# Step-size projection of the Mamba-2 layer: fp32 on four 32-column groups of TensorE and a stacked identity, in place of a slab whose columns are repeated four times

## Chip, cores and metric

The kernel runs on one core of one Trainium2 chip. The metric is the device time of one execution in microseconds (us), as the median of several runs. Lower is better.

## What is computed

The reference is one inference step of a two-layer streaming encoder: layer 0 mixes tokens by chunked band attention, layer 1 by a Mamba-2 scan, and a dense MLP follows each. There are 512 prompt tokens and 64 sample tokens, so 576 columns in all, in two halves of 288. The change concerns one product in layer 1, the 32 columns of the input projection that give each head its step size.

```python
proj = x @ w_in                                  # 1024 -> z, x/B/C, dt
z = proj[..., :D_INNER]
xbc = proj[..., D_INNER:D_INNER + CONV_CH]
dt_raw = proj[..., D_INNER + CONV_CH:]           # 32 columns, one per head
...
dt = jax.nn.softplus((dt_raw + dt_bias).astype(jnp.float32)).reshape(bsz, t, g, r)
a = -jnp.exp(a_log.astype(jnp.float32)).reshape(g, r)
y, h = _ssd_scan(xs, dt, a, bm, cm, h0)
```

## The kernel before

**Weights.** `Weights` walks through 223 slabs of 128x1024 in the order of `weight_plan`. SyncE's queue (SP) loads each into one of four raw buffers `wr`. `split` makes two fp32r halves of it, `wh` by a ScalarE cast (L182) and `wl` by a VectorE subtraction (L183), in one of five pairs of buffers. Every large product is then three fp32r matmuls for each of eight slices of the inner dimension: `wh` by `xh`, `wh` by `xl`, `wl` by `xh`. `dense` (L308) does both halves of the tokens for each weight, `dense_half` (L338) one half only.

**The order of the work.** The program is written in one sequence, and the scheduler of the language places the instructions of each engine in an order of its own, by readiness and priority; an engine then works through its list in order. Two helpers interleave: `side.start` takes a generator, and `side.tick` runs a piece of it every so many matmuls. So a layer norm runs in pieces between matmuls. A step whose result is used late can still be queued early.

**The place of the change.** `in_proj(0)` (from L917) begins the Mamba layer. For half 0 and then half 1 it computes dt (32 columns, `dense_half([dtw], h)`), c and b, then x0 and x1 of the first group. The slab `dt` holds the 32 columns four times side by side, so that it has 128 like all others; only the first 32 rows of its product are used. Half 0 begins while the layer norm of half 1 still runs as side work:

- `layer_norm` (L396) takes sums that GpSimd has made (L393), forms the mean by an fp32 matmul with a constant matrix (L401), squares on ScalarE (L408), adds the squares on VectorE (L412, L413), and gets the scale through `split_stats` (L362) and `bcast` (six matmuls, L372). VectorE multiplies it in (L423), ScalarE adds gain and bias tile by tile (L429, which gives `x32`), ScalarE or VectorE casts to `xh` (L434, L436), and VectorE forms `xl` (L437).
- `dt_in` (L985, VectorE) adds the bias, once for each half. `dt_chain` (L990 to L1004) is the softplus on 32 partitions by 576 columns, one exponential on ScalarE (L991) and some 16 VectorE instructions. The scheduler interleaves them with the convolution steps on VectorE (`conv`, L913).
- The gate slabs z0 and z1 follow (`gate_in`, `dense`), and with z1 as side work `dt_rest`: ten transposes of dt and dt times a on TensorE (L1010, L1011), cumulative sums (L1017, L1018), and the exponentials. The scan of the groups follows (L1071, L1087, L1102), with the projections of the next groups between.

```python
dt_in(dense_half([dtw], h)[0], h)
if h == 1:
    W.drop()
    dt_chain()
```

Of the kernel before, what the change touches and what calls it, by code (L numbers as in the profile page):

```python
# [5 lines left out]
F32 = mybir.dt.float32  # L6
# [7 lines left out]
P = 128  # L14
# [3 lines left out]
HALF = 288  # L18
# [16 lines left out]
PM_ID = PM_D + 16  # L35
# [75 lines left out]
def build(nc, io):  # L111
    from contextlib import ExitStack
    plan = weight_plan()
    with tile.TileContext(nc) as tc, ExitStack() as es:
        V, S, PE, GP, SY = nc.vector, nc.scalar, nc.tensor, nc.gpsimd, nc.sync
# [9 lines left out]
        def tmp(w=NT):  # L125
            return tp.tile([P, w], F32, name="tmp", tag="tmp")
# [4 lines left out]
        def mmt():  # L131
            return pmm.tile([P, 1024], F32, name="mm", tag="mm")
# [11 lines left out]
        x32 = xp.tile([P, 8, NT], F32, name="x32")  # L144
# [3 lines left out]
        class Weights:  # L148
# [37 lines left out]
            def produce(self, i):  # L186
                p = plan[i]
                r = self.raw_free
                if p[0] != "ups":
                    self.split(i, self.raw.pop(r))  # L190
                    self.raw_free += 1
                    return
                r1, r2 = self.raw[r], self.raw[r + 1]
                lo, hi = slice(0, HALFK), slice(HALFK, 1024)
                eng = V if p[2:4] == (0, PLAIN // 2) else GP
                if p[4] == 2:
                    eng.tensor_tensor(out=r2[:, lo], in0=r1[:, lo], in1=r2[:, lo], op=ALU.subtract)  # L197
                    self.split(i, r2)
                    eng.tensor_tensor(out=r2[:, hi], in0=r2[:, hi], in1=r2[:, lo], op=ALU.subtract)  # L199
                    eng.tensor_tensor(out=r2[:, lo], in0=r1[:, lo], in1=r2[:, hi], op=ALU.add)  # L200
                elif p[4] == 4:
                    self.split(i, r2[:, lo])
                elif p[4] == 1:
                    self.split(i, r1)
                    eng.tensor_tensor(out=r1[:, hi], in0=r1[:, hi], in1=r2[:, hi], op=ALU.subtract)
                else:
                    self.split(i, r2[:, hi], r1[:, hi])
                    del self.raw[r], self.raw[r + 1]
                    self.raw_free += 2
                    self.prefetch()  # L210
# [78 lines left out]
        pm = cst.tile([P, PM_N], F32, name="pm")  # L289
# [41 lines left out]
        def dense_half(ws, h):  # L331
            ps = mmt()
            outs = [ps[:, 512 * j:512 * j + HALF] for j in range(len(ws))]
            for k in range(8):
                for w, o in zip(ws, outs):
                    wh, wl = wk(w)(k)
                    for i, (a, b) in enumerate(((wh, xh), (wh, xl), (wl, xh))):
                        PE.matmul(o, a, b[:, k, h * HALF:(h + 1) * HALF],  # L338
                                  start=k == 0 and i == 0, stop=k == 7 and i == 2)
                    side.tick(3)  # L340
            return outs

        def wk(w, n=128, off=0):
            return lambda k: (w[0][:, k * n + off:k * n + off + 128], w[1][:, k * n + off:k * n + off + 128])
# [537 lines left out]
        def ssm():  # L882
            cumd = dr.tile([32, NT], F32, name="cumd")
            expd = dr.tile([32, NT], F32, name="expd")
            with tc.tile_pool(name="ssm", bufs=2) as ap:
                tok = ap.tile([P, 5, 64], F32, name="tok", bufs=1)
                win = ap.tile([P, 5, 32], F32, name="win", bufs=1)
                cumt = ap.tile([P, 5, 32], F32, name="cumt", bufs=1)
# [31 lines left out]
                def in_proj(g):  # L920
                    items = [("c", g, 24 + g, "c"), ("b", g, 16 + g, "b"), ("x", 2 * g, 2 * g, "x0"),
                             ("x", 2 * g + 1, 2 * g + 1, "x1")]
                    out = []
                    if g == 0:
                        ws, xr = [], []
                        dtw = W.get("dt")
                        for h in range(2):
                            if h == 0:
                                side.start(layer_norm(1, 1, False), LN_EVERY)
                            else:  # L930
                                side.drain()
                            dt_in(dense_half([dtw], h)[0], h)
                            if h == 1:
                                W.drop()
                                dt_chain()
                            for i0 in range(0, 4, PAIR_IN):
                                if h == 0:
                                    for i in range(i0, i0 + PAIR_IN):
                                        ws.append(W.get(*items[i][:2]))
                                        xr.append(xpad4(i))  # L940
                                        conv_pre(xr[i], items[i][2])
                                for i, src in zip(range(i0, i0 + PAIR_IN), dense_half(ws[i0:i0 + PAIR_IN], h)):
                                    conv_in(xr[i], src, h * HALF, (h + 1) * HALF)
                                    if h == 1:
                                        W.drop()
                                        out.append(conv(xr[i], items[i][2], items[i][3]))
                        out.append(gate_in(0, 0))
                        side.start(dt_rest(), DE)
                        out.append(gate_in(0, 1))
                        side.drain()  # L950
                        return out
                    res = {}
                    for (kind, j) in GORD:
                        if kind == "z":
                            res["z", j] = gate_in(g, j)
                            continue
                        _, idx, ct, tag = items[{"c": 0, "b": 1, "x": 2 + j}[kind]]
                        w = W.get(kind, idx)
                        xr = xpad()
                        conv_pre(xr, ct)  # L960
                        ps = mmt()
                        dense(ps, wk(w), ax_h, ax_l, 8, (0, 1))
                        conv_in(xr, ps[:, PS0:PS0 + NT], 0, NT)
                        W.drop()
                        res[kind, j] = conv(xr, ct, tag)
                    return [res[k] for k in (("c", 0), ("b", 0), ("x", 0), ("x", 1), ("z", 0), ("z", 1))]
# [10 lines left out]
                def xpad4(i):  # L977
                    if i < 2:
                        return xpad()
                    return ap.tile([P, 2, NT], F32, name="yy", tag="yy", bufs=2).rearrange("p a b -> p (a b)")[:, 0:582]  # L980

                dtt = [ap.tile([P, NT], F32, name=f"dt{i}", tag=("yh", "yl")[i % 2], bufs=4)[0:32] for i in range(4)]

                def dt_in(src, h):
                    V.tensor_scalar(out=dtt[0][:, h * HALF:(h + 1) * HALF], in0=src[0:32], scalar1=hpm[:, 0:1],  # L985
                                    scalar2=None, op0=ALU.add)

                def dt_chain():
                    xr, e, q, p = dtt
                    V.scalar_tensor_tensor(out=e, in0=xr, scalar=-1.0, in1=xr, op0=ALU.mult, op1=ALU.max)  # L990
                    S.activation(e, e, AF.Exp, scale=-1.0)  # L991
                    V.tensor_scalar(out=xr, in0=xr, scalar1=0.0, scalar2=None, op0=ALU.max)
                    V.tensor_scalar(out=q, in0=e, scalar1=2.0, scalar2=None, op0=ALU.add)
                    V.reciprocal(q, q)
                    V.tensor_tensor(out=e, in0=e, in1=q, op=ALU.mult)
                    V.tensor_tensor(out=q, in0=e, in1=e, op=ALU.mult)
                    V.tensor_scalar(out=p, in0=q, scalar1=1.0 / 15.0, scalar2=None, op0=ALU.mult)
                    for c in (13, 11, 9, 7, 5, 3):
                        V.scalar_tensor_tensor(out=p, in0=p, scalar=1.0 / c, in1=q, op0=ALU.add, op1=ALU.mult)
                    V.scalar_tensor_tensor(out=p, in0=p, scalar=1.0, in1=e, op0=ALU.add, op1=ALU.mult)  # L1000
                    V.scalar_tensor_tensor(out=p, in0=p, scalar=2.0, in1=xr, op0=ALU.mult, op1=ALU.add)
                    na = sp.tile([32, 1], F32, name="na", tag="na", bufs=1)
                    S.activation(na, hpm[:, 1:2], AF.Exp)
                    V.tensor_scalar(out=q, in0=p, scalar1=na, scalar2=-1.0, op0=ALU.mult, op1=ALU.mult)  # L1004
# [293 lines left out]
```

## Time and profile before

| | |
|---|---|
| median of 3 runs | 1705.39 us (1703.11 to 1706.24) |
| the profiled execution, its own time | 1701.69 us |
| its span in the trace | 1699.9 us |
| mean granted TensorE clock | 0.991 |
| TensorE matmul (PE) busy | 97% |
| TensorE weight load (PEld) busy | 93% |
| VectorE (DVE) busy | 63% |
| ScalarE (ACT) busy | 46% |
| GpSimd (POOL) busy | 22% |

The profile is taken from one execution, whose own time lies a little below the runs'. The span goes from the first to the last recorded instruction. A share of busy time is an average over the whole span; a stage of 25 us can look quite different. A granted clock of 1.00 is 2.4 GHz, 0.50 is 1.2 GHz.

### The profile page before, as it was taken

How to read it: one execution, taken by the hardware profiler on the slowest of the kernel's cores; microseconds unless marked ns; L12 is line 12 of the kernel's file. 1: busy time of each engine (PE TensorE's matmuls, PEld its weight loads, DVE VectorE, ACT ScalarE, POOL GpSimd, SP SyncE). 2: the span in 40 equal slices, each digit the busy share in tenths (PEclk: the TensorE clock that was granted, in tenths of full speed). 3: DMA queues.
4: the chain of work that ended last, by engine and by line, in shares of the span. 5: the costliest groups of instructions: out<-in, count | busy, mean ns of one | idle time of the engine just before them, and what ended most of it. 6: DMA issues, size and time to landing. Idle time of an engine off the chain costs nothing. (4 is left out here: it accounts for less than half of the span.)

```text
span 1699.9 us, 30804 instructions
## 1 busy us (share of the span) xinstructions
PE 1652.7 (97%) x12545; PEld 1576.5 (93%) x12545; DVE 1064.4 (63%) x1879; ACT 774.8 (46%) x1278; POOL 378.1 (22%) x412
## 2 busy tenths in 40 slices
PE   9999999899999999989999999999998999999995
PEld 8888887899999999989899999999988999999995
DVE  6555556784362736477875775777778637364446
ACT  5433443374261716246663563565326616254332
POOL 0000000211312212206541340344220212131211
PEclk9999999999999999999999999999999999999998
DMA  8333332114131313113332332333211313223121
GB/s 272 106 119 113 111 105 72 62 30 133 51 125 51 123 52 127 61 66 119 117 104 87 103 99 89 99 103 110 68 57 36 125 50 111 64 75 124 52 73 56
DMA packets 76925, 157.22 MB, mean 92 GB/s; under 512 B 11440, under 2 KB 40240, under 8 KB 76784
## 3 DMA queue, kind: packets, MB, share of 16 engines
q1 hardware_dynamic: 76784, 155.25, 28.2%
q8 instruction: 99, 1.62, 0.4%
q14 instruction: 42, 0.34, 0.1%
HBM read 145.80 MB, written 9.42 MB: 91 GB/s over the span
## 5 line engine op out<-in xcount | busy, mean ns | idle before, releaser
L182 ACT CAST wh<-wr 128x1024 fp32r<-128x1024 f32 (+1 forms) x301 | 280.7, 938 | 472.3 <-PE mm L308 362.0
L183 DVE TENSOR_TENSOR wl<-wr,wh 128x1024 fp32r<-128x1024 f32 (+1 forms) x301 | 359.9, 1200 | 106.1 <-ACT wh L182 100.9
L308 PE MATMUL mm<-xh,wl 128*128 128x288 f32 x1088 | 237.8, 299 | 0.0
L308 PE MATMUL mm<-xh,wh 128*128 128x288 f32 x1088 | 237.5, 300 | 0.1
L308 PE MATMUL mm<-xl,wh 128*128 128x288 f32 x1088 | 237.4, 299 | 0.0
L308 PE MATMUL mm<-hh,wl 128*128 128x288 f32 x960 | 222.0, 297 | 0.0
L308 PE MATMUL mm<-hl,wh 128*128 128x288 f32 x960 | 221.7, 296 | 0.0
L308 PE MATMUL mm<-hh,wh 128*128 128x288 f32 x960 | 221.7, 296 | 0.0
L384 DVE TENSOR_TENSOR x<-x,mm 128x288 f32<-128x288 f32 (+1 forms) x112 | 64.5, 580 | 196.2 <-PE mm L308 185.1
L308 PEld LDWEIGHTS mm<-xl,wh 128*128 128x128 f32 x1088 | 174.3, 189 | 4.1 <-issue 3.8
L308 PEld LDWEIGHTS mm<-xh,wh 128*128 128x128 f32 x1088 | 174.5, 188 | 2.6 <-issue 1.4
L308 PEld LDWEIGHTS mm<-xh,wl 128*128 128x128 f32 x1088 | 174.3, 189 | 1.5
L308 PEld LDWEIGHTS mm<-hh,wl 128*128 128x128 f32 x960 | 160.1, 188 | 0.1
L308 PEld LDWEIGHTS mm<-hh,wh 128*128 128x128 f32 x960 | 160.1, 188 | 0.1
L308 PEld LDWEIGHTS mm<-hl,wh 128*128 128x128 f32 x960 | 160.1, 188 | 0.0
L541 PE MATMUL ax<-xh,wh 128*128 128x288 f32 x416 | 123.1, 296 | 0.5 <-ACT ut L559 0.4
L541 PE MATMUL ax<-xl,wh 128*128 128x288 f32 x416 | 122.6, 295 | 0.0
L541 PE MATMUL ax<-xh,wl 128*128 128x288 f32 x416 | 122.5, 294 | 0.0
L197 POOL TENSOR_TENSOR wr<-wr 128x512 f32<-128x512 f32 x24 | 40.7, 1695 | 337.9 <-DMA wr<-in_wts 297.8
L913 DVE SCALAR_TENSOR_TENSOR tmp<-xpad,pm,tmp 128x579 f32<-128x579 f32 x90 | 88.9, 988 | 1.5 <-ACT tmp L911 0.8
L338 PE MATMUL mm<-xh,wh 128*128 128x288 f32 x240 | 72.8, 307 | 8.3 <-DVE xh L434 5.1
L541 PEld LDWEIGHTS ax<-xh,wh 128*128 128x128 f32 x416 | 78.1, 188 | 1.6 <-ACT ut L559 1.3
(267 smaller groups left out, 3503.2 us busy)
## 6 DMA issues: line engine op xcount, KB each, us to landing
wr<-in_wts SPq DMA_DIRECT2D x223, 512.0 KB, 3.4
cumb<-cumd SPq DMA_DIRECT2D x32, 256.0 KB, 3.8
e<-expd SPq DMA_DIRECT2D x48, 64.0 KB, 3.5
tb<-in_rel SPq DMA_DIRECT2D x16, 160.0 KB, 3.0
out_k<-tmp SPq DMA_DIRECT2D x8, 288.0 KB, 2.5
out_v<-tmp SPq DMA_DIRECT2D x8, 288.0 KB, 2.1
tb<-in_rel SPq DMA_DIRECT2D x16, 144.0 KB, 2.9
ts<-in_rel SPq DMA_DIRECT2D x16, 144.0 KB, 3.0
```

What stands on the lines that cost most here:

```text
L182: S.copy(hi[:, sl], raw)
L183: V.tensor_tensor(out=lo[:, sl], in0=raw, in1=hi[:, sl].bitcast(F32), op=ALU.subtract)
L197: eng.tensor_tensor(out=r2[:, lo], in0=r1[:, lo], in1=r2[:, lo], op=ALU.subtract)
L308: PE.matmul(ps[:, o:o + HALF], w, a(k)[:, t0:t0 + HALF], start=first and i == 0, stop=last and i == 2)
L338: PE.matmul(o, a, b[:, k, h * HALF:(h + 1) * HALF], start=k == 0 and i == 0, stop=k == 7 and i == 2)
L384: V.tensor_tensor(out=dst, in0=dst, in1=src, op=ALU.add)
L541: chain(PE.matmul(out, a, b, start=not more and k == 0 and i == 0, stop=k == 3 and i == 2, skip_group_check=True), k or i or name != "t3")
L913: V.scalar_tensor_tensor(out=acc, in0=xr[:, k:k + 579], scalar=col(k), in1=acc, op0=ALU.mult, op1=ALU.add)
```

## The change

The `dt` slab is no longer split. Its raw fp32 buffer is multiplied as it stands, with the fp32 `x32` instead of `xh` and `xl` (`dt_proj`, new). Each of the eight slices of the inner dimension uses 32 columns of the slab as weights and writes to one of four groups of 32 partitions of a PSUM tile, slice k to group k modulo 4, so that each group sums two slices. ScalarE then copies the four partial sums to SBUF, and a matmul with `stack`, four 32x32 identities one under the other, adds them. `stack` is loaded by four small DMAs on SP's queue ahead of the layer. The bias add takes its input from this last product.

```diff
--- before.py
+++ after.py
@@ -186,6 +186,10 @@
             def produce(self, i):
                 p = plan[i]
                 r = self.raw_free
+                if p[0] == "dt":
+                    self.t[i] = self.raw.pop(r)
+                    self.raw_free += 1
+                    return
                 if p[0] != "ups":
                     self.split(i, self.raw.pop(r))
                     self.raw_free += 1
@@ -883,6 +887,9 @@
             cumd = dr.tile([32, NT], F32, name="cumd")
             expd = dr.tile([32, NT], F32, name="expd")
             with tc.tile_pool(name="ssm", bufs=2) as ap:
+                stack = ap.tile([P, 32], F32, name="stack", bufs=1)
+                for j in range(4):
+                    SY.dma_start(stack[32 * j:32 * j + 32, :], io["pm"][0:32, PM_ID:PM_ID + 32])
                 tok = ap.tile([P, 5, 64], F32, name="tok", bufs=1)
                 win = ap.tile([P, 5, 32], F32, name="win", bufs=1)
                 cumt = ap.tile([P, 5, 32], F32, name="cumt", bufs=1)
@@ -929,7 +936,7 @@
                                 side.start(layer_norm(1, 1, False), LN_EVERY)
                             else:
                                 side.drain()
-                            dt_in(dense_half([dtw], h)[0], h)
+                            dt_in(dt_proj(dtw, h), h)
                             if h == 1:
                                 W.drop()
                                 dt_chain()
@@ -980,6 +987,19 @@
                     return ap.tile([P, 2, NT], F32, name="yy", tag="yy", bufs=2).rearrange("p a b -> p (a b)")[:, 0:582]
 
                 dtt = [ap.tile([P, NT], F32, name=f"dt{i}", tag=("yh", "yl")[i % 2], bufs=4)[0:32] for i in range(4)]
+
+                def dt_proj(w, h):
+                    sl = slice(h * HALF, (h + 1) * HALF)
+                    ps = mmt()
+                    for k in range(8):
+                        j = k % 4
+                        PE.matmul(ps[32 * j:32 * j + 32, 0:HALF], w[:, 128 * k:128 * k + 32], x32[:, k, sl],
+                                  start=k < 4, stop=k > 3)
+                    parts = tmp()[:, 0:HALF]
+                    S.copy(parts, ps[:, 0:HALF])
+                    out = ps[0:32, 512:512 + HALF]
+                    PE.matmul(out, stack, parts, start=True, stop=True)
+                    return out
 
                 def dt_in(src, h):
                     V.tensor_scalar(out=dtt[0][:, h * HALF:(h + 1) * HALF], in0=src[0:32], scalar1=hpm[:, 0:1],
```

In the changed file the lines below the first hunk are four further down (L308 is L312, L338 is L342, L372 is L376, L401 is L405), and behind the second hunk seven: the convolution steps L920, the 32-column matmuls L996, the copy L999, the stacked identity L1001, the bias add L1005, the softplus L1010 to L1024, the transposes L1030 and L1031.

**TensorE, half 0.** Below is TensorE's order where the projection of half 0 begins, before. `mm_8050` is the MLP of layer 0, `mm_8126` dt, `mm_8182` c and b, `ax2_8142` the mean of the second layer norm half.

```order
L308 MATMUL mm_8050<-hh_7449,wl_7780 128x288
L338 MATMUL mm_8126<-xh_79,wh_8104 128x288
L338 MATMUL mm_8182<-xh_79,wh_8110 128x288
L401 MATMUL ax2_8142<-tmp_7679,invd_166 128x288
L338 MATMUL mm_8126<-xl_80,wh_8104 128x288
L338 MATMUL mm_8126<-xh_79,wl_8105 128x288
L338 MATMUL mm_8126<-xh_79,wh_8104 128x288
L338 MATMUL mm_8126<-xl_80,wh_8104 128x288
```

With the change `mm_8127` is dt and `mm_8152` c and b:

```order
L312 MATMUL mm_8050<-hh_7449,wl_7780 128x288
L996 MATMUL mm_8127<-x32_78,wr_7684 32x288 x4
L342 MATMUL mm_8152<-xh_79,wh_8111 128x288
L405 MATMUL ax2_8168<-tmp_7679,invd_166 128x288
L996 MATMUL mm_8127<-x32_78,wr_7684 32x288
L342 MATMUL mm_8152<-xl_80,wh_8111 128x288
L342 MATMUL mm_8152<-xh_79,wl_8112 128x288
L996 MATMUL mm_8127<-x32_78,wr_7684 32x288
L342 MATMUL mm_8152<-xh_79,wh_8117 128x288
L342 MATMUL mm_8152<-xl_80,wh_8117 128x288
L342 MATMUL mm_8152<-xh_79,wl_8118 128x288
L996 MATMUL mm_8127<-x32_78,wr_7684 32x288
```

Four of the eight products stand together ahead of the mean matmul; the other four stand one by one among the products of c and b, with the eighth nine matmuls behind the seventh, and the stacked identity seven behind the eighth. In half 1 the pattern is much the same.

**TensorE ahead of the dt transposes.** Before, 180 matmuls stand between the last dt product and the first transpose; the last of them belong to z1 (`mm_8605`):

```order
L308 MATMUL mm_8605<-xl_80,wh_8532 128x288 x2
L308 MATMUL mm_8605<-xh_79,wl_8533 128x288 x2
L308 MATMUL mm_8605<-xh_79,wh_8532 128x288 x2
L308 MATMUL mm_8605<-xl_80,wh_8532 128x288 x2
L1010 MATMUL ax1_8646<-pm_162,dt3_8101 128x32
L1011 MATMUL ax1_8646<-pm_162,dt2_8100 128x32
```

With the change there are 128 between the second stacked identity and the first transpose. `mm_8523` is z0, `mm_8580` z1, `mm_8688` c of the next group:

```order
L312 MATMUL mm_8523<-xl_80,wh_8501 128x288 x2
L312 MATMUL mm_8523<-xh_79,wl_8502 128x288 x2
L312 MATMUL mm_8580<-xh_79,wh_8507 128x288 x2
L312 MATMUL mm_8580<-xl_80,wh_8507 128x288 x2
L312 MATMUL mm_8688<-xh_79,wh_8513 128x288 x2
L312 MATMUL mm_8688<-xl_80,wh_8513 128x288 x2
L1030 MATMUL ax1_8621<-pm_162,dt3_8106 128x32
L1031 MATMUL ax1_8621<-pm_162,dt2_8105 128x32
```

Nearly all of z1 now stands behind the transposes, starting with its first product by the low half `wl_8508`.

**VectorE, the softplus chain.** Before, two splits of weight slabs stand inside the chain, for z0 and z1:

```order
L985 TENSOR_SCALAR dt0_8098<-mm_8333,hpm_164 32x288
L990 SCALAR_TENSOR_TENSOR dt1_8099<-dt0_8098 32x576
L183 TENSOR_TENSOR wl_8527<-wr_8114,wh_8526 128x1024
L992 TENSOR_SCALAR dt0_8098<-dt0_8098 32x576
L993 TENSOR_SCALAR dt2_8100<-dt1_8099 32x576
L994 RECIPROCAL dt2_8100<-dt2_8100 32x576
L183 TENSOR_TENSOR wl_8533<-wr_8120,wh_8532 128x1024
L995 TENSOR_TENSOR dt1_8099<-dt1_8099,dt2_8100 32x576
```

With the change the split of z0 stands ahead of the chain and that of z1 behind it, at its end:

```order
L920 SCALAR_TENSOR_TENSOR tmp_8491<-yy_8224,pm_162,tmp_8491 128x579
L1021 SCALAR_TENSOR_TENSOR dt3_8106<-dt3_8106,dt0_8103 32x576
L920 SCALAR_TENSOR_TENSOR tmp_8491<-yy_8224,pm_162,tmp_8491 128x579
L1024 TENSOR_SCALAR dt2_8105<-dt3_8106,na_8350 32x576
L183 TENSOR_TENSOR wl_8508<-wr_8121,wh_8507 128x1024
L183 TENSOR_TENSOR wl_8514<-wr_8140,wh_8513 128x1024
```

All twelve convolution steps of the first group are now inside the chain, eleven before.

## Rows read from the trace of the kernel before

**Rows 1.** Page, busy time; then by stage: us, busy PE PEld DVE ACT POOL, PEclk, DMA, GB/s.

```profile
PE 1652.7 (97%) x12545; PEld 1576.5 (93%) x12545; DVE 1064.4 (63%) x1879; ACT 774.8 (46%) x1278; POOL 378.1 (22%) x412
760.00:785.00 25.00, 25.00 (x194) 24.79 (x193) 24.97 (x32) 15.03 (x29) 19.32 (x8) 1.00 0.13 44
785.00:1220.00 435.00, 432.43 (x3357) 410.83 (x3357) 318.71 (x568) 231.26 (x362) 155.17 (x207) 1.00 0.33 103
```

**Rows 2.** The chain that ended last: start us, us, what.

```profile
1624.70 12.80 PE mm L317 x96
1661.77 0.48 PE ax L401 x2
```

**Rows 3.** PE's timeline, 732 to 759: start us, us, instruction [idle before <-releaser].

```profile
733.53 0.82 PE L338 MATMUL mm<-xh,wh 128*128 128x288 f32 x2 [2.55 <-DVE xh L434]
735.21 1.33 PE L401 MATMUL ax<-tmp,invd 128*128 128x288 f32 x2 [0.86 <-POOL tmp L393]
...
749.13 0.91 PE L372 MATMUL ax<-pm,y 96*128 96x96 f32 x6
...
754.38 0.30 PE L338 MATMUL mm<-xh,wh 128*128 128x288 f32 x1
...
758.66 0.29 PE L338 MATMUL mm<-xh,wl 128*128 128x288 f32 x1
```

**Rows 4.** POOL's timeline, the last sum of the second layer norm half.

```profile
733.98 1.17 POOL L393 TENSOR_TENSOR tmp<-tmp,x 128x288 f32<-128x288 f32 x1 [2.14 <-DVE x L384]
```

**Rows 5.** ACT's timeline, the first five normalised tiles of each half.

```profile
731.84 2.70 ACT L429 ACTIVATE x<-x,pm 128x288 f32<-128x288 f32 x5
...
750.87 2.71 ACT L429 ACTIVATE x<-x,pm 128x288 f32<-128x288 f32 x5 [2.87 <-DVE x L423]
```

**Rows 6.** Busy time by stage where the granted clock is low.

```profile
735.50:738.50 3.00, 3.00 (x12) 2.71 (x12) 3.00 (x5) 2.97 (x6) 0.00 (x0) 0.50 0.41 122
```

**Rows 7.** Timelines of DVE and, last row, ACT: the softplus chain's ends.

```profile
758.99 0.51 DVE L985 TENSOR_SCALAR dt<-mm,hpm 32x288 f32<-32x288 f32 x1 [1.06 <-PE mm L338]
759.53 0.75 DVE L990 SCALAR_TENSOR_TENSOR dt<-dt 32x576 f32<-32x576 f32 x1
760.21 1.21 DVE L183 TENSOR_TENSOR wl<-wr,wh 128x1024 fp32r<-128x1024 f32 x1
...
765.86 1.15 DVE L183 TENSOR_TENSOR wl<-wr,wh 128x1024 fp32r<-128x1024 f32 x1
...
782.03 0.50 DVE L1004 TENSOR_SCALAR dt<-dt,na 32x576 f32<-32x576 f32 x1
782.46 0.81 DVE L913 SCALAR_TENSOR_TENSOR tmp<-yy,pm,tmp 128x579 f32<-128x579 f32 x1
...
760.31 0.68 ACT L991 ACTIVATE dt<-dt 32x576 f32<-32x576 f32 x1 [0.40 <-DVE dt L990]
```

**Rows 8.** PE's timeline in the attention: products on 64 columns among full ones.

```profile
60.97 0.43 PE L308 MATMUL mm<-xh,wh 128*128 128x288 f32 x2
61.33 0.44 PE L819 MATMUL ax<-pt,v 128*64 128x128 f32 x4
61.70 0.53 PE L308 MATMUL mm<-xl,wh 128*128 128x288 f32 x2
...
76.02 1.09 PE L819 MATMUL ax<-pt,v 128*64 128x128 f32 x16
77.05 0.55 PE L797 MATMUL ax<-pm,s 128*128 128x128 f32 x3
```

**Rows 9.** PE's timeline at the first dt transpose.

```profile
782.52 0.43 PE L308 MATMUL mm<-xl,wh 128*128 128x288 f32 x2
782.88 0.24 PE L1010 MATMUL ax<-pm,dt 32*128 32x32 f32 x1
```

**Rows 10.** PE's timeline, its waits in the first steps of the scan.

```profile
806.03 0.66 PE L1102 MATMUL ax<-mt,xdt 128*64 128x128 f32 x8 [0.46 <-DVE mt L1087]
...
808.37 0.49 PE L1071 MATMUL ax<-oc,ob 128*128 128x128 f32 x2 [1.06 <-DVE mt L1087]
```

## The prediction

> **What bounds the kernel now.** The page's first part and the busy time by stage come first [rows 1]: TensorE (PE) is busy 97% of the span, from 785 to 1220 us for 432.4 of 435 us. Time that PE loses in the projection is therefore not made up later, since PE has no slack behind it. The same view shows what is special here: from 760 to 785 us VectorE (DVE) is full too, 24.97 of 25 us. The chain that ended last prices PE [rows 2]: 96 fp32r matmuls of 288 columns in 12.80 us, 0.133 us each, and an fp32 matmul of that size (two records) in 0.48 us.
>
> **The window of the change, before.** PE's timeline [rows 3] starts the first projection matmul at 733.53, after 2.55 us without work, then stands again until the mean matmul (L401) at 735.21, which waits for GpSimd's last sum (733.98 + 1.17) [rows 4]. ScalarE (ACT) makes the normalised x32, five tiles in 2.70 us from 731.84, so one each 0.54 us [rows 5]. The granted clock is 0.50 from 735.5 to 738.5 [rows 6], 1.2 GHz instead of 2.4, after PE had mostly stood since 731; 12 matmuls ran in those 3 us.
>
> **Removed and moved at no cost.** The dt slab's split (1.21 us of DVE [rows 7] and a cast on ACT) goes: both engines waited for PE around it. The four stack loads are issued ahead of the projection and first needed behind half 0's products; the load of the scan's first state behind them in SP's queue slips by four issues and is needed only in the scan. The slab keeps its raw buffer until the last half-1 product, so one load waits on PE near 760; before, that load waited for the split at 760.21 [rows 7], so it is no later. The copy of the partial sums (288 columns, about 0.4 us) has seven matmuls, 0.9 us, as cover. Were a cover gone, the cost is the duration named. The bias add of half 0 now stands in DVE's queue ahead of the squares of the second layer norm half and holds them until the stack product. By my count their sum is ready some 0.6 us before PE asks for it: no cost, but if the product comes a us later, a us is lost.
>
> **PE's matmuls.** Removed: 48 x 0.133 = 6.4 us. Added: per half, eight 32-column products and the stacked identity. The order shows that only the first four stand together; the other four and the stack product are visits of one matmul among 128-column ones. No fp32 matmul on 32 columns is in this trace; the nearest is the 64-column product of attention [rows 8]. Two matmuls at 60.97 should be issued by 61.24, the pair of products starts at 61.33, the next full matmul at 61.70: 0.46 us for two products. Sixteen records (eight products) take 1.03 us, so six more cost 0.66, 0.22 a pair. A visit thus has 0.24 us besides its work. A solo is 0.48 + 0.24 = 0.72 us. The lower end is 0.48 (no cost of changing), the upper 0.96 (the visit's cost doubled, or the low clock [rows 6]); I take 0.72 because the 64-column row is the same kind of visit.
>
> Half 0: the four grouped products get their tiles from 732.4 on, 0.54 us apart, longer than one takes; they fit ahead of the mean matmul and cost nothing (0.7 or more if GpSimd's sum did not hold PE there anyway). The one removed matmul that stood there saves nothing: +0.1. Four solos and the stack product: 5 x 0.72 = +3.6.
>
> Half 1: in the order 12 matmuls instead of 34 stand between the broadcasts of the layer norm and the group. Before, the first tile was ready 2.28 us after the broadcasts began (750.87 + 0.54 less 749.13) [rows 3, 5]. PE now arrives at about that moment, so the group is paced by ACT: three intervals of 0.54 and the last product, 2.3 us. ACT then has two copies and a cast in its queue before tile 4: PE waits about 0.5 more. Five visits are 3.6. Together 6.4 us. Before, the 24 matmuls and four others ran from 754.38 to 758.95 [rows 3], 4.57 us for 28 x 0.133 = 3.7, so 0.9 of waiting goes with them.
>
> Until the end of the second stack product (call it T): -6.4 + 0.1 + 3.6 + 6.4 - 0.9 = +2.8. The clock: the 12 slow matmuls cost 12 x 0.11 = 1.3 us. PE now starts a us earlier and may keep 2.4 GHz (-1.3), or fall again (0). I take half: -0.6. Lag at T, against the work that PE has done by then: +2.2 us.
>
> **The wait that is new.** From T, DVE runs the softplus chain and PE what does not depend on it. Before, DVE began at 758.99 and ended the chain at 782.53 [rows 7]; 180 PE matmuls stood in that place and ended at 782.78, so the transposes at 782.88 waited for nothing to speak of [rows 9]. In the change's order only 128 stand there, 17.0 us, because the low half of the second gate slab (z1) is split behind the chain, no longer inside it. DVE's chain: 23.54 less two splits (1.21 + 1.15), plus a twelfth convolution step (0.81), plus about 0.4 for the exponential, which no split covers any more (0.75 + 0.68 before the next step can start [rows 7]): 22.4 us. PE stands 22.4 - 17.0 = **5.4 us** in front of the transposes. Behind them it needs z1's low half, 1.15 us after the chain against 0.7 of transposes: +0.4. Nothing downstream gives it back, PE being full [rows 1].
>
> Sum: 2.2 + 5.4 + 0.4 = **+8.0 us**. The profiled execution took 1701.69 us (span 1699.92 and 1.8 around it), 3.7 below the median of the runs; on it that is 1709.7, on the median 1705.39 it is **1713.4**. About 0.2% (3.4 us) is what a measurement of this kernel can tell from no change. With solos at 0.48 and the clock kept it is 8.0 - 2.4 - 0.7 = +4.9, with 0.96 and the clock falling +11.
>
> **Rivals.**
> *Solos overlap their neighbours.* If eight products cost two rounds of four, as the design says, six visits go (6 x 0.72 = 4.3): +3.7, 1709.1. For it: the pairs of [rows 8] do run together. Against: the neighbours here use all columns. The Trainium skill, TensorE: Matmul & The Clock Gate, section "Part 3: Packing small matmuls", says that matmuls on distinct column groups run concurrently, the span being about one of them plus some 4 ns a tile; the pairs agree, four at once no run here shows, and by that rule alone the projection would be cheaper than before.
> *Clock or visits dearer.* The clock falls later or stays at 1.2 GHz while narrow products run: each visit 0.96 or more and other matmuls at 0.24 instead of 0.133. Against: the stretch was 3 us [rows 6]. About +13, 1718.
> *Partly given back.* PE waited 0.46 and 1.06 us at 806 to 808 in the first scan [rows 10]; later PE work might fill both (-1.5). With the overlap above: +2.2, 1707.6, no change to speak of.
> *Faster.* The place is DVE's chain: ahead of the transposes it has two splits fewer. If it took 17.0 us or less there, the whole wait (5.4 + 0.4) would vanish; with the overlap of the first rival (-4.3) and the clock kept (-0.7) T would come 2.8 earlier than before (2.2 - 4.3 - 0.7), and with the waits at 806 to 808 gone (-1.5) it is -4.3, 1701.1. It decides at 17.0 us. Against: the chain's instructions, all in the trace, add up to 22.
>
> **How the numbers follow.** Forecast 0.57, overlap 0.12, dearer 0.10, partly given back 0.10, faster 0.11. Slower by over 0.2%: the first three less 0.05 for the overlap's lower half, 0.74; within: 0.10 + 0.05 = 0.15; faster: 0.11. The forecast's own range is 1710 to 1717 (its +4.9 to +11); the range reaches to the overlap and to the given-back case less the runs' spread of some 3 us (1704.5) and to the dearer case (1718), leaving out the faster case and half the dearer, 0.16.
>
> **What would show it.** PE standing about 5 us ahead of the dt transposes, "waited for DVE dt"; solos about 0.7 us apart from what follows; the half-1 group paced by ACT; the second bias add about 5 us later than 758.99 (20 more convolution-input matmuls lie ahead of it); stage 785 to 1220 as before but shifted. Wrong: no wait ahead of those transposes, solos that cost 0.3 us or over 1 us, a low clock that lasts beyond 3 us, or a new wait for a weight load.

## The result and the profile after

With the change the kernel takes 1715.2 us (median of 6 runs, 1713.45 to 1719.02) against 1705.58 us before (6 runs, 1703.11 to 1706.24). The ratio is 1.007, 95% interval 1.0058 to 1.0082: slower, as forecast (1713.4, range 1704.5 to 1718). The medians lie 9.6 us apart; the ratio of the runs, with its interval, stands for 10 to 14 us.

The page of the profile shows nothing of it. TensorE's share of busy time is 97% as before [rows 1]:

```profile
PE 1663.5 (97%) x12533; PEld 1577.5 (92%) x12533; DVE 1065.0 (62%) x1878; ACT 771.6 (45%) x1277; POOL 369.9 (22%) x412
```

The stages do. Busy time by stage of the changed kernel (columns as in rows 1), the stretch with the dt transposes, the one where the scan starts, and the long rest of the layer:

```profile
780.00:790.00 10.00, 5.43 (x30) 4.93 (x31) 10.00 (x14) 1.55 (x4) 10.00 (x3) 0.66 0.21 63
806.00:818.00 12.00, 9.82 (x54) 7.74 (x53) 7.95 (x13) 3.94 (x7) 11.25 (x12) 0.72 0.54 138
830.00:1220.00 390.00, 390.00 (x3031) 373.72 (x3031) 285.97 (x498) 205.14 (x322) 128.12 (x180) 1.00 0.32 98
```

From 780 to 790 TensorE works 5.43 of 10 us, at a mean granted clock of 0.66, while VectorE has no gap. From 806 to 818 the clock is low again. The kernel before, whose scan starts some 4 us earlier, has a granted clock of 1.00 there:

```profile
806.00:818.00 12.00, 10.92 (x84) 8.52 (x85) 8.33 (x21) 10.13 (x14) 10.64 (x11) 1.00 0.44 111
```

After 830 nothing is lost. TensorE's timeline of the changed kernel, in six places: a layer norm just ahead of the change, one visit (a single narrow product among full ones), the transposes, the first cumulative sum, the scan's first wait, and a layer norm after all of it:

```profile
728.22 0.91 PE L376 MATMUL ax<-pm,y 96*128 96x96 f32 x6 [0.53 <-DVE y L361]
...
758.28 0.29 PE L342 MATMUL mm<-xl,wh 128*128 128x288 f32 x1
758.50 0.67 PE L996 MATMUL mm<-x,wr 128*32 128x288 f32 x2
759.11 0.40 PE L342 MATMUL mm<-xh,wl 128*128 128x288 f32 x1
759.34 0.29 PE L342 MATMUL mm<-xh,wh 128*128 128x288 f32 x1
759.47 0.29 PE L342 MATMUL mm<-xl,wh 128*128 128x288 f32 x1
...
784.26 0.31 PE L1030 MATMUL ax<-pm,dt 32*128 32x32 f32 x1 [3.64 <-DVE dt L1021]
785.43 0.31 PE L1031 MATMUL ax<-pm,dt 32*128 32x32 f32 x1 [0.86 <-DVE dt L1024]
...
786.56 0.85 PE L312 MATMUL mm<-xh,wl 128*128 128x288 f32 x2
...
789.59 0.43 PE L312 MATMUL mm<-xh,wl 128*128 128x288 f32 x2
...
793.86 0.30 PE L1037 MATMUL ax<-tok,pm 128*128 128x32 f32 x2
...
810.13 1.12 PE L1122 MATMUL ax<-mt,xdt 128*64 128x128 f32 x8 [2.01 <-DVE mt L1107]
...
852.38 1.48 PE L376 MATMUL ax<-pm,y 96*128 96x96 f32 x12
```

The two layer norms, which serve as landmarks, and the first cumulative sum of the kernel before:

```profile
729.38 0.91 PE L372 MATMUL ax<-pm,y 96*128 96x96 f32 x6 [0.53 <-DVE y L357]
...
787.56 0.30 PE L1017 MATMUL ax<-tok,pm 128*128 128x32 f32 x2
...
841.34 1.58 PE L372 MATMUL ax<-pm,y 96*128 96x96 f32 x12 [0.67 <-DVE y L357]
```

Between the landmarks the stretch grew from 111.96 to 124.16 us, by 12.2, which is the whole difference of the two spans (1712.2 less 1699.9). VectorE's timeline dates the chain:

```profile
762.94 0.50 DVE L1005 TENSOR_SCALAR dt<-mm,hpm 32x288 f32<-32x288 f32 x1 [3.20 <-PE mm L1001]
...
784.87 0.50 DVE L1024 TENSOR_SCALAR dt<-dt,na 32x576 f32<-32x576 f32 x1
785.30 4.61 DVE L183 TENSOR_TENSOR wl<-wr,wh 128x1024 fp32r<-128x1024 f32 x4
```

- **Lag at the second bias add.** It comes at 762.94 instead of 758.99, counted from the first landmark 5.11 us later. In the order 20 more products of c and b lie ahead of it, 2.66 us. So 2.4 us are lost by then.
- **The wait ahead of the transposes.** 3.64 us for the chain's p and 0.86 for the product behind it, and 0.2 just before for z0's buffer: 4.7 us of idle time. Counted from start to start it is more: from 762.83 to the second transpose (785.43) 22.6 us pass for 128 full products (17.0 us), 5.6 lost, where the kernel before loses 0.2 over its 180; that makes 5.4. Chain and convolution steps take VectorE from 762.94 to 785.3, and four splits stand in a row behind them, z1's the first.
- **The clock behind the wait.** From 786.56 to 789.59 twelve full matmuls take 3.03 us, 0.25 each instead of 0.133 (1.4 us), and the transposes take some 0.4 us more than before. The granted clock fell to 1.2 GHz inside the wait of 3.64 us, at about 782.7, and was back at 2.4 GHz from about 789.5.
- **The scan.** From the first cumulative sum to the second landmark 58.52 us pass against 53.78 before, with 18 more full products among them (2.4 us, counted in the two timelines): 2.4 us are lost there. The wait at 810.13 is 2.01 us (before 0.46 and 1.06 [rows 10]), and behind it the clock is low again. With 2.4, 5.4 and 1.8 from above this makes 12.0 of the 12.2.

### The profile page after: what moved, and what is told of

Same layout as the page of the kernel before. It is cut to its first block, busy times and chain, and to the rows that moved or that the text cites. A ratio compares the mean times of both kernels' runs of the same rounds, so it can differ in the third digit from the quotient of the medians.

```text
span 1712.2 us, 30786 instructions
## 1 busy us (share of the span) xinstructions
PE 1663.5 (97%) x12533; PEld 1577.5 (92%) x12533; DVE 1065.0 (62%) x1878; ACT 771.6 (45%) x1277; POOL 369.9 (22%) x412
## 5 line engine op out<-in xcount | busy, mean ns | idle before, releaser
L312 PE MATMUL mm<-xh,wh 128*128 128x288 f32 x1088 | 238.9, 301 | 0.4 <-ACT z L980 0.2
L312 PE MATMUL mm<-xh,wl 128*128 128x288 f32 x1088 | 238.6, 300 | 0.1
L312 PE MATMUL mm<-xl,wh 128*128 128x288 f32 x1088 | 238.2, 300 | 0.0
L312 PE MATMUL mm<-hh,wl 128*128 128x288 f32 x960 | 222.0, 297 | 0.0
L312 PE MATMUL mm<-hl,wh 128*128 128x288 f32 x960 | 221.7, 296 | 0.0
L312 PE MATMUL mm<-hh,wh 128*128 128x288 f32 x960 | 221.7, 296 | 0.0
L312 PEld LDWEIGHTS mm<-xl,wh 128*128 128x128 f32 x1088 | 175.0, 189 | 4.2 <-issue 3.8
L312 PEld LDWEIGHTS mm<-xh,wh 128*128 128x128 f32 x1088 | 175.6, 189 | 3.1 <-issue 1.4
L312 PEld LDWEIGHTS mm<-xh,wl 128*128 128x128 f32 x1088 | 175.2, 190 | 1.6 <-DVE wl L183 0.2
L312 PEld LDWEIGHTS mm<-hh,wl 128*128 128x128 f32 x960 | 160.1, 188 | 0.1
L312 PEld LDWEIGHTS mm<-hh,wh 128*128 128x128 f32 x960 | 160.1, 188 | 0.1
L312 PEld LDWEIGHTS mm<-hl,wh 128*128 128x128 f32 x960 | 160.1, 188 | 0.0
L920 DVE SCALAR_TENSOR_TENSOR tmp<-xpad,pm,tmp 128x579 f32<-128x579 f32 x90 | 90.4, 1005 | 0.7
L545 PEld LDWEIGHTS ax<-xl,wh 128*128 128x128 f32 x416 | 78.1, 188 | 0.0
```

Source lines behind the costliest of these rows:

```text
L312: PE.matmul(ps[:, o:o + HALF], w, a(k)[:, t0:t0 + HALF], start=first and i == 0, stop=last and i == 2)
L545: chain(PE.matmul(out, a, b, start=not more and k == 0 and i == 0, stop=k == 3 and i == 2, skip_group_check=True), k or i or name != "t3")
L920: V.scalar_tensor_tensor(out=acc, in0=xr[:, k:k + 579], scalar=col(k), in1=acc, op0=ALU.mult, op1=ALU.add)
```

## The experiments

The runs were timed against the kernel before on the same chip, whose median was 1703.35 to 1703.87 us in these sessions; ratios are used throughout. 0.001 is 1.7 us.

### The order of one split

**z1's split inside the chain.** The narrow products stay as the change has them; only the place of z1's split in VectorE's order is put back: `dt_chain` becomes a generator with a `yield` behind `V.reciprocal`, and the rest of it is written behind the loading of z1.

```diff
-                                dt_chain()
+                                rest = dt_chain()
+                                next(rest)
...
                                         W.drop()
+                                        if i == 0:
+                                            W.load(W.pos + 2)
+                                            next(rest, None)
```

> Edit: the softplus chain is written in two pieces, with the split of the gate slab z1 between them, so VectorE makes z1's low half inside the chain, as before the change; narrow products and stacked identity stay. In the order 165 matmuls instead of 128 then stand between the second stacked identity and the first dt transpose. Theory (order): the wait of 3.64 + 0.86 us ahead of the transposes shrinks below 0.5 and the granted clock does not fall there (about 2.1 us of work at half speed from 785.4 to 789.8), so 1715.2 - 4.5 - 2.1 = 1708.6; if the scan's wait of 2.0 us and its stretch at half clock go with it, about 1705.5. Rival (visits): the narrow products make the loss and the wait only shows it, so 1714 to 1716.

Ratio 1.0019 (1.0011 to 1.0028): 8.7 us of the 11.9 come back, by an edit that touches no product. Its busy time by stage and the places of the waits on TensorE:

```profile
780.00:790.00 10.00, 9.99 (x77) 9.35 (x76) 10.00 (x15) 2.40 (x6) 10.00 (x6) 1.00 0.18 58
806.00:818.00 12.00, 10.48 (x71) 8.37 (x70) 6.76 (x15) 8.53 (x11) 10.38 (x10) 0.86 0.43 114
```

```profile
784.49 0.24 PE L1035 MATMUL ax<-pm,dt 32*128 32x32 f32 x1
...
808.24 0.66 PE L1127 MATMUL ax<-mt,xdt 128*64 128x128 f32 x8 [0.47 <-DVE mt L1112]
```

No wait ahead of the transposes, full clock from 780 to 790, and the scan's first wait is 0.47 us, about that of the kernel before.

**The same split behind the chain, in the kernel before.** The counter-test: no narrow product anywhere. `after_chain` ties an instruction behind the chain's last one (L1004) in VectorE's order.

```diff
+                    sub = V.tensor_tensor(out=lo[:, sl], in0=raw, in1=hi[:, sl].bitcast(F32), op=ALU.subtract)
+                    if plan[i] == ("z", 1):
+                        after_chain(sub)
```

> Edit to the kernel before, with its three fp32r products and no narrow matmul: z1's split is tied behind the last instruction of the softplus chain on VectorE, as the change's order had it. In the order 148 matmuls instead of 180 then stand ahead of the dt transposes, 19.7 us against 22.6 us of chain (23.54 less one split). Theory (order): TensorE waits about 2.9 us there and 0.4 for z1's low half, ratio 1.0019; if the granted clock falls behind the wait too, about 2 us more, 1.0031. Rival: without the narrow products the order of one split costs nothing, since later work takes the place: 1.0000.

Ratio 1.0039 (1.0027 to 1.0051), 6.6 us, above both figures. TensorE's timeline shows waits of 1.48, 0.92 and 1.19 us instead of 3.3 together, and the scan's wait of 2.19:

```profile
780.65 0.24 PE L1019 MATMUL ax<-pm,dt 32*128 32x32 f32 x1 [1.48 <-DVE dt L1010]
781.82 0.24 PE L1020 MATMUL ax<-pm,dt 32*128 32x32 f32 x1 [0.92 <-DVE dt L1013]
...
783.68 0.83 PE L317 MATMUL mm<-xh,wl 128*128 128x288 f32 x2 [1.19 <-DVE wl L190]
...
807.61 1.12 PE L1111 MATMUL ax<-mt,xdt 128*64 128x128 f32 x8 [2.19 <-DVE mt L1096]
```

```profile
780.00:790.00 10.00, 7.24 (x46) 7.03 (x47) 8.72 (x11) 1.83 (x3) 7.25 (x4) 0.83 0.50 154
806.00:818.00 12.00, 10.23 (x56) 8.30 (x56) 8.42 (x16) 5.84 (x10) 9.48 (x12) 0.72 0.45 129
```

The order of one split costs 6.6 us by itself. The waits in front of the scan are 3.6 of it; the low clock and the longer wait of the scan stand beside the rest, and no run divides it between them.

**The convolutions behind the chain.** Another way to have the chain end earlier, on the change:

```diff
+                        x = V.scalar_tensor_tensor(out=acc, in0=xr[:, k:k + 579], scalar=col(k), in1=acc,
+                                                   op0=ALU.mult, op1=ALU.add)
+                        if ct in (24, 16, 0, 1):
+                            after_chain(x)
```

> Edit: the change, with the convolution steps of the first group tied behind the softplus chain on VectorE (the splits stand inside it then; 160 matmuls, 21.3 us, ahead of the transposes against some 20 us of VectorE). Another way to take the wait away. Theory (the wait is VectorE's, whatever fills it): as the first run, ratio 1.0019. Rival: the convolutions come 12 x 0.8 = 9.6 us later than the chain and TensorE waits for them at the scan instead: 1.004 or more.

Ratio 1.0021 (1.0011 to 1.0031), the same as the first run within the intervals. The wait ahead of the transposes is gone here too, and the granted clock is 1.00 from 780 to 790 and from 806 to 818:

```profile
783.73 0.24 PE L1039 MATMUL ax<-pm,dt 32*128 32x32 f32 x1
```

It is the wait for VectorE that costs, whatever is taken out of its way.

### The clock

**A filler in the wait.** Nine products whose results are overwritten:

```diff
+                    for _ in range(9):
+                        PE.matmul(pt[:, 0:HALF], ident, z[:, 0:HALF], start=True, stop=True)
```

> Edit: the change as it is, with nine fp32 products of 288 columns (identity by z0, result overwritten; 9 x 0.48 = 4.3 us) in TensorE's order ahead of the dt transposes, where it waits. Nothing the kernel computes depends on them. Theory (clock): the wait stays, but TensorE works through it, the granted clock stays at 2.4 GHz until the scan, and the 2.1 us of half speed from 785.4 to 789.8 come back: 1713.1. Rival: the fall of the clock does not come from the idle stretch, or the filler delays the transposes by as much: 1715 to 1716.

Ratio 1.0055 (1.0042 to 1.0067), median 1712.51. Against the change that is 0.0015, 2.6 us, where 2.1 were expected; but the two intervals overlap, and by the medians, each against the kernel before on its own chip, it is 0.5 us (9.2 above it, 9.6 with the change). The trace tells it better: the filler stands in the wait, the clock from 780 to 790 is 1.00 where it was 0.66, and between the landmarks 122.3 us pass instead of 124.2. Part of the gain is lost again in the scan, which waits 2.38 and 1.16 us here (2.01 and 0.17 in the change), with a low clock behind the second wait.

```profile
780.29 4.63 PE L1030 MATMUL ax<-z,pm 128*128 128x288 f32 x18 [0.21 <-ACT z L980]
...
809.64 0.66 PE L1124 MATMUL ax<-mt,xdt 128*64 128x128 f32 x8 [2.38 <-DVE mt L1109]
```

```profile
780.00:790.00 10.00, 9.26 (x55) 7.70 (x55) 10.00 (x13) 1.79 (x5) 10.00 (x2) 1.00 0.20 63
```

With work that nobody needs in the wait, the matmuls behind it ran at 2.4 GHz. That the whole kernel became faster by it is likely, and not clear of the noise.

**A narrow filler.**

```diff
+                    for i in range(16):
+                        j = 32 * (i % 4)
+                        PE.matmul(pt[j:j + 32, 0:HALF], ident[:, 0:32], z[:, 0:HALF], start=True, stop=True)
```

> Edit: as the filler, but with sixteen fp32 products on 32 columns, in turn on the four column groups, all ready at the same time. It measures whether four groups run together. Overlap: 16 x 0.48 / 4 = 1.9 us for all sixteen, 0.12 apart. No overlap: 16 x 0.48 = 7.7 us, which is 3 us longer than the wait that it stands in, so the time is about 1718. The clock: if narrow products keep it, no stretch at half clock from 783 to 790; if only full ones do, it falls as without a filler.

```profile
781.03 2.15 PE L1031 MATMUL ax<-z,pm 128*32 128x288 f32 x32 [0.21 <-ACT z L980]
783.11 0.53 PE L312 MATMUL mm<-xh,wh 128*128 128x288 f32 x2
...
785.48 0.24 PE L1033 MATMUL ax<-pm,dt 32*128 32x32 f32 x1 [1.57 <-DVE dt L1021]
786.64 0.31 PE L1034 MATMUL ax<-pm,dt 32*128 32x32 f32 x1 [0.92 <-DVE dt L1024]
...
788.42 0.68 PE L312 MATMUL mm<-xh,wh 128*128 128x288 f32 x2
```

Sixteen products take 2.08 us, 0.13 each against 0.48 alone: the four column groups run together. They fill only half of the wait, and 1.57 and 0.92 us stay. The clock falls as without a filler (a pair takes 0.68 us at 788.42, 0.53 at 783.11), and the ratio is 1.0088 (1.0073 to 1.0104), no better than the change's 1.007. The median, 1718.65 us, is the figure that was expected for no overlap, but the trace shows another reason: the granted clock is 0.50 from 786 to 792, again from about 799 to 803, though TensorE has no idle time from 790 to 806, and from about 817 to 822. Why it falls at 799 no run shows. Whether narrow products hold the clock is not told apart, since TensorE stood behind them.

### What a narrow product costs

**One column group, no stacked identity.**

```diff
-                        PE.matmul(ps[32 * j:32 * j + 32, 0:HALF], w[:, 128 * k:128 * k + 32], x32[:, k, sl],
-                                  start=k < 4, stop=k > 3)
+                        PE.matmul(ps[0:32, 0:HALF], w[:, 128 * k:128 * k + 32], x32[:, k, sl], start=k == 0, stop=k == 7)
```

> Edit: all eight narrow products of a half accumulate in one column group; the copy, the stacked identity and its loads go. In the order of this kernel z1's split stands inside the chain without further edit (175 matmuls ahead of the dt transposes), so no wait there. Theory: what is left of the loss is visits, 0.70 us each; against the first run (ratio 1.0019, 3.3 us above before) two visits go, -1.4: ratio 1.0011. Rival: the four groups overlap among the narrow products and so save time in this kernel; then this run is slower than the first one by two to four times 0.48 us: ratio 1.0025 to 1.003.

Ratio 1.0011 (1.0001 to 1.002). The four groups as the change has them bring nothing: without them, without the copy and the identity, the kernel is 1.4 us faster than the first run, though the intervals overlap.

**The same with 128 columns.**

```diff
-                        PE.matmul(ps[0:32, 0:HALF], w[:, 128 * k:128 * k + 32], x32[:, k, sl], start=k == 0, stop=k == 7)
+                        PE.matmul(ps[:, 0:HALF], w[:, 128 * k:128 * k + 128], x32[:, k, sl], start=k == 0, stop=k == 7)
```

> Edit: as the one before, but each product uses all 128 columns of the raw slab (still fp32, one group, no stacked identity). The order is the same, instruction by instruction. Theory: 0.22 us of the 0.70 of a visit is the change between 32 and 128 columns, so a visit takes 0.48 here and eight to twelve of them save 1.8 to 2.6 us against the run before: ratio about 1.0000. Rival: the 0.22 belongs to fp32 after fp32r, or to weight loads, and stays or grows with four times the columns: ratio as before, 1.0011, or above.

Ratio 0.9999 (0.999 to 1.0008): four times as many columns, and 2.0 us less. The two intervals overlap, but the traces agree: between the landmarks 109.4 us pass with 128 columns and 111.4 with 32. One visit with 32 columns, then one with 128, on TensorE's timeline:

```profile
736.71 0.30 PE L342 MATMUL mm<-xh,wh 128*128 128x288 f32 x1
736.93 0.67 PE L992 MATMUL mm<-x,wr 128*32 128x288 f32 x2
737.53 0.40 PE L342 MATMUL mm<-xl,wh 128*128 128x288 f32 x1
737.77 0.29 PE L342 MATMUL mm<-xh,wl 128*128 128x288 f32 x1
```

```profile
737.59 0.29 PE L342 MATMUL mm<-xh,wh 128*128 128x288 f32 x1
737.72 0.65 PE L992 MATMUL mm<-x,wr 128*128 128x288 f32 x2
737.99 0.51 PE L342 MATMUL mm<-xl,wh 128*128 128x288 f32 x1
738.34 0.30 PE L342 MATMUL mm<-xh,wl 128*128 128x288 f32 x1
738.47 0.29 PE L342 MATMUL mm<-xh,wh 128*128 128x288 f32 x1
```

From the first to the last start of the narrow case 1.06 us pass, two full matmuls (0.27) among them: the visit takes 0.79. In the wide case 0.88 with three (0.40): 0.48, no more than the product itself. The change between 32 and 128 columns thus costs 0.31 us a visit. The Trainium skill, TensorEngine Tiling (Array Packing), section "Key Properties", says that changing the tiling mode, and not just the tile, drains the engine; the two rows agree, as only the narrow product pays more than its own time.

**Narrow products together.** Half 0's projection moved to half 1's, with z1's split inside the chain:

```diff
-                            dt_in(dt_proj(dtw, h), h)
                             if h == 1:
+                                dt_in(dt_proj(dtw, 0), 0)
+                                dt_in(dt_proj(dtw, 1), 1)
```

> Edit: z1's split inside the chain as in the first run of this set, and the step-size projection of half 0 is written directly ahead of that of half 1, so that in TensorE's order sixteen narrow products stand together and then both stacked identities; no visit of a single product among full ones is left. Overlap: sixteen products in 1.9 us, paced in part by ScalarE's tiles, and about 1.6 us for the identities and the uncovered copy; the narrow work falls from some 9 us to 4, so 4 to 5 us below the first run, 1702 to 1705. No overlap: 7.7 us and 1.6, about the same as the first run, 1708 to 1709.

Ratio 1.0008 (0.9999 to 1.0017), 1704.75 us: 1.9 us below the first run, where overlap should have given 4 to 5. The overlap is there, but half 1's group has to wait:

```profile
753.55 1.18 PE L1001 MATMUL mm<-x,wr 128*32 128x288 f32 x16
756.36 2.24 PE L1001 MATMUL mm<-x,wr 128*32 128x288 f32 x14 [1.63 <-ACT yy L905]
759.01 0.67 PE L1001 MATMUL mm<-x,wr 128*32 128x288 f32 x2 [0.42 <-ACT x L433]
759.29 0.67 PE L1006 MATMUL mm<-tmp,stack 128*32 128x288 f32 x2
```

Half 0's eight take 1.18 us from 753.55; half 1's stand 1.63 us behind ScalarE, are paced by its tiles and stand 0.42 us more. The scan waits longer too, 1.60 and 1.47 us instead of the first run's 0.47 and 1.06.

**Narrow products together, in the middle of c and b.** `dense_half` calls back behind slice 3 (products) and slice 5 (identity):

```diff
+                                def mid(k):
+                                    if k == DT_AT[h]:
+                                        dtp[h] = dt_proj(dtw, h)
...
+                                    if k == DT_SUM[h]:
+                                        dt_in(dt_sum(*dtp[h]), h)
```

> Edit: the change with the eight narrow products of each half written in the middle of c and b (behind slice 3) and the stacked identity behind slice 5, so that the eight stand together with seven or more matmuls to cover the copy; z1's split inside the chain. From the sixteen filler products in 2.08 us: eight take 1.04, plus 0.24 for the change of columns, plus 0.70 for the identity, 2.0 a half instead of 3.2 for the 24 fp32r products: -2.4 us. Ahead of the transposes 164 matmuls (21.8 us) stand against about 23 us of VectorE, a wait of 1 us. Theory (adjacent products overlap): ratio 0.999 to 1.000. Rival (narrow products wait for ScalarE's tiles wherever they stand): 1.001 to 1.002.

A miss: 1.0034 (1.0023 to 1.0045). The group is as cheap as expected, but what now stands in its old place waits for the layer norm instead:

```profile
753.71 0.37 PE L344 MATMUL mm<-xh,wh 128*128 128x288 f32 x1 [1.03 <-DVE xh L442]
754.95 0.40 PE L344 MATMUL mm<-xl,wh 128*128 128x288 f32 x1 [0.87 <-DVE xl L445]
...
758.21 1.18 PE L1010 MATMUL mm<-x,wr 128*32 128x288 f32 x16
...
809.13 0.66 PE L1140 MATMUL ax<-mt,xdt 128*64 128x128 f32 x8 [1.79 <-DVE mt L1125]
```

Ahead of the transposes 0.30 and 0.92 us of waiting are left, about the 1 us expected. This profile's own execution took 1706.94 us, the median of its runs 1709.89. What the other runs lose beyond it no trace shows, and it stays open.

### A version that beats both

**Both halves in one slab.** From the kernel before: the slab has its 32 columns four times, so columns 32 to 63 can hold the low half. One weight then serves `xh` and `xl`, and two fp32r products a slice do what three did. z1's split is kept inside the chain.

```diff
+                    S.copy(w, raw)
+                    V.tensor_tensor(out=k3(w, 32), in0=k3(raw, 0), in1=k3(w, 0).bitcast(F32), op=ALU.subtract)
...
+                        for x in (xh, xl):
+                            PE.matmul(ps[:, 0:HALF], w[:, 128 * k:128 * k + 128], x[:, k, h * HALF:(h + 1) * HALF],
+                                      start=k == 0 and x is xh, stop=k == 7 and x is xl)
...
+                    V.tensor_tensor(out=o, in0=o, in1=src[32:64, 0:HALF], op=ALU.add)
```

> Edit to the kernel before: the 128 columns of the step-size slab hold the high half in columns 0 to 31 and the low half in 32 to 63 (columns 64 up are copies of no use), so two fp32r products for each slice (by xh and by xl) instead of three, with one weight for both; VectorE subtracts 256 elements instead of 1024 and adds the two row groups. z1's split is put inside the chain as in the first run. 48 products become 32: -16 x 0.133 = -2.1 us, ratio 0.9988, if the rest stays. Rival: the time is set by what follows (VectorE's chain), since the bias add needs a second step and the chain starts no earlier: ratio 1.000.

Ratio 0.9985 (0.9976 to 0.9994), median 1700.94 us: 2.6 us faster than the kernel before. There is no narrow product and no copy of partial sums, and TensorE works 10.00 of 10 us from 780 to 790.

**With the convolutions behind the chain as well** (the tie shown above; here it alone keeps z1's split ahead of the chain's end).

> Edit: the kernel with both halves in one slab (0.9985) and the convolution steps tied behind the chain as in the run before. If the dt transposes and so the sums and loads of the scan come earlier, the scan's waits (0.21 and 1.06 us in the profile of 0.9985) shrink: 0.9978 to 0.9985. Rival: the late convolutions hold up the scan: 1.000 or more.

Ratio 0.9983 (0.9973 to 0.9993), median 1701.22: no difference from the one before. The scan's waits shrink as expected, to 0.57 us at its second step and none at its first; no gain in time can be told from it. The late convolutions do not hold up the scan.

## Why the prediction was right, point by point

- **Visits.** Put at 0.72 us, measured 0.79. The mechanism (a fixed cost of a narrow product among full ones, 0.24 by the 64-column rows) held; the size is 0.31. The prediction found no fp32 matmul on 32 columns in the trace of before, but five transposes on 32 columns stand there among full products (L1032, at 790.94). From 790.81 to 791.87 they take 0.79 us; at 0.11 each, as the full-width transposes at 793.20 follow one another, that leaves 0.24 as well, so the price would have been the same. Undoing it by width alone moved the time by 2.0 us.
- **Half 1's group paced by ScalarE.** It runs from 752.96 at ScalarE's pace, with a wait of 0.48 behind it. The forecast of 6.4 us for all of half 1 compares with 6.7 (second stacked identity done at 762.9, group begun at 752.96, less 24 products of c and b).
- **Lag at the second bias add.** Put at 2.2, found 2.4; the bias add was expected 5 us later than before and came 5.1 us later from the landmark.
- **The wait ahead of the transposes.** Put at 5.4 and 0.4 for z1's low half; 4.7 and about 0.1 were found as idle time, 5.4 from start to start. The chain took 22.4 us as forecast, from 762.94 to 785.37. The wait itself is shorter because TensorE lost 0.2 us at z0's buffer before it, and because the first transpose needs only p, which is there at 784.2.
- **What the sum left out.** "Nothing downstream gives it back" was right but not enough: downstream took more. The term that is missing is the granted clock behind the wait (1.8 us with the transposes) and the scan with its second slow stretch (2.4 us). One of the prediction's own signs of being wrong, a low clock that lasts beyond 3 us, did come: 1.2 GHz from about 782.7 to 789.5 and from 810.0 to 816.5. The prediction weighed the clock only in the projection, at half of 1.3 us. There the slow stretch came earlier, from about 731.6 to 734.9, on the four narrow products (2.72 us, in the first run at full clock 2.23), and from 735 on the clock was 1.00, where before it was 0.50 from 735.5 to 738.5; what that was worth no run separates. So the traces show 12.2 us against the 8.0 forecast, the medians 9.6: the profiled execution of the kernel before lies 3.9 us below the median of its runs, that of the change at its median. That the forecast of 1713.4 lies only 1.8 us from the median is therefore in part luck: the sum lacked some 4 us of what the traces show.
- **The rivals.** "Solos overlap" fell for this kernel: it needs the products side by side, as in the fillers (0.13 each), and the order doesn't place them so. By the rule of the Trainium skill, TensorE: Matmul & The Clock Gate, section "Part 3: Packing small matmuls", that matmuls on distinct column groups run concurrently, the projection would have been cheaper; the narrow filler's row agrees with the rule, and the changed kernel's visits are narrow products that have no neighbour to run with. "Faster" fell: VectorE's chain took 22.4 us, not 17.0. "Partly given back" fell: the waits of the scan grew.

Shown by runs: that the split's order makes most of the loss (put back 1.0019, put in alone 1.0039), that the clock stays at 2.4 GHz when the wait is filled (filler), and what a change of columns costs. Only argued: how the 2.4 us in the scan divide between its longer wait and its low clock. Why the scheduler put the split behind the chain stays open. The run with one column group, which has neither copy nor stacked identity nor their loads, kept it inside without any edit of the chain, so one of these differences moved it.

## What to carry to other kernels

Where an engine is full and another chain runs beside it, count the work that stands between a result and its first use in the new order: a change that saves 30 matmuls can lose more by one instruction that moves behind a chain. Small products are cheap side by side (eight in 1.18 us) and dear one by one among large ones (0.79 us each); even so, neither order tried here that put them side by side beat the kernel before (1.0008 and 1.0034). Filling the unused columns did (0.9985). A wait of some us on TensorE costs more than its length when the work behind it runs at 1.2 GHz.

## What was not expected of the hardware

- A wait's price grew beyond its length: 3.6 us of waits in front of the scan in the kernel before with the moved split made 6.6 us in all, and a useless filler of 4.63 us in the wait of the changed kernel kept the clock up behind it and shortened the stretch between the landmarks by 1.9 us.
- The first run and the kernel before have nearly the same waits in the scan (0.47 against 0.46 us at the first), yet the first run's clock is 0.86 from 806 to 818, and before it is 1.00 throughout that stage. In the projection the changed kernel and the one with the filler have the same instructions and the same wait of 1.53 us, yet from 732 to 735 the granted clock is 0.51 in the one profile and 1.00 in the other. And behind the narrow filler it fell at 799 without any idle time. The waits alone do not tell when the clock falls.
- An fp32 product on all 128 columns among fp32r products takes 0.48 us and on 32 columns 0.79.
